# Row pitch and start address of the moved operands in a two-block transformer kernel

## The chip, the cores and the metric

The kernel runs on one core of a Trainium2 chip. The metric is the device time of one execution in microseconds, from the first to the last instruction of the program with what lies around it; the median of several runs is quoted.

## What is computed

Two blocks of transformer layers follow each other on one sequence of 256 tokens and 1024 features, all in float32. The first block has four layers (two pooling mixers, one neighbourhood attention, one convolution) and also carries a context of 256 tokens for a while. The second block has two layers, and each of them is:

```python
x = x + 0.5 * swiglu_ffn(x, ffn1_norm[l], ffn1_w_gate[l], ffn1_w_up[l], ffn1_w_down[l])   # 1024 -> 2816 -> 1024
h = rms_norm(x, mix_norm[l])
aq, ak, av, bq, bk, bv, cq, ck, cv, cg, gates = jnp.split(h @ w_in[l], split_points, axis=-1)
...                                     # three attentions: y_a, y_b, y_c, 512 features each
merged = (g[:, :, 0] * (y_a @ w_branch_a[l]) + g[:, :, 1] * (y_b @ w_branch_b[l])
          + g[:, :, 2] * (y_c @ w_branch_c[l]))
x = x + merged @ w_out[l]
x = x + 0.5 * swiglu_ffn(x, ffn2_norm[l], ffn2_w_gate[l], ffn2_w_up[l], ffn2_w_down[l])
```

## The kernel before

**Three matmuls for one product.** Every large product is made of two parts of each operand. A weight tile (`raw`, 4 rows of 128 by 256 columns, or two such rows) is loaded by a DMA of SP's queue, ScalarE casts it into a high part `whi` (line 162), and VectorE subtracts that from it for a low part `wlo` (line 163). Activations are split in the same way (`split`, lines 341 and 342; `operand`, lines 1157 and 1158). A product of a 128x128 weight square with 256 tokens is then three matmuls of 256 columns that add up in one PSUM half bank: high by high, high by low, low by high (`mm3`; the matmul itself is line 257, called from everywhere). A "triple" below means these three. In the feature-major form (`fm_unit`) the weight square is stationary and the activations are moved: `HH` and `HL`, `UH` and `UL`, `OH` and `OL`. In the token-major form (`tm_unit`, used by `project`) the activations are stationary and the weights `whi`, `wlo` are moved. In the profile's names "mm<-HH,whi" moves HH against stationary whi, and "mm<-whi,HH" moves whi.

**The tiles of activations.** `HH` and `HL` are long-lived tiles of 8 rows (one for each 128 features) of 544 floats, that is 2176 bytes. Columns 0 to 255 of a row hold the normalised input of the layer; columns 288 to 543 are called `YH` and `YL` and hold what the mixers hand to their output product. The first block also uses columns up to 511 (two times 256 tokens) and columns 256 and 257 (a shift). The second block reads 256 columns at a time: all rows of HH in the up products of the feed-forward parts (`ffn`, 22 chunks of 8 rows by 2 squares by 3 matmuls) and in the products of the mixer (`mix`), and four rows of YH for a branch matrix or eight for the output matrix. `UH` and `UL` (22 rows of 256 floats) hold the inner features of a feed-forward part and are moved in its down product; `OH` and `OL` (8 rows of 256 floats) are the same for the last layer of the first block.

**Where they begin.** By the allocator's addresses, modulo 256 bytes: HH and HL begin at 128, so with 2176 bytes a row their rows begin at 128 and 0 in turn, and those of YH at 0 and 128 in turn. UH, UL, OH and OL begin at 0 in every row. The split weights `whi` and `wlo` begin at 192 in every row and square (a tile of 8 floats, `pad_w`, lies ahead of them). Below, "a 0 row" or "a 128 row" is one whose moved operand begins there.

**What sets the order.** The kernel is scheduled by hand. A list `units` holds weight tiles and other work in the order of use. `get` hands out the next tile and lets splits run up to five tiles ahead (`fill`); five raw buffers are loaded ahead of that. Work that hangs on a product (norms, attention steps) is put in by `later` (after so many estimated microseconds of matmuls) and `beside` (steps of a generator at a rate). The second block is `ffn`, `mix`, `ffn` for each of two layers. In a feed-forward part the sums of the norm interrupt the stream of matmuls twice near its start (`norm_a`, `norm_b`); from there to its end it runs through. In the mixer, attention steps stand between chunks of matmuls.

The tiles and the views that are read:

```python
    HH = per.tile([P, KD, 544], F32R, name="HH")
    HL = per.tile([P, KD, 544], F32R, name="HL")
    YH, YL = HH[:, :, 288:544], HL[:, :, 288:544]
    def hx(n):
        return lambda k: HH[:, k, 0:n]
            fp.tile([P, 16], F32, name="pad_u")
            UH = fp.tile([P, KF, 256], F32R, name="UH")
```

Of the kernel before, what the change touches and what calls it, by code (L numbers as in the profile page):

```python
# [114 lines left out]
def kernel(ctx: ExitStack, tc: tile.TileContext, I, csmall, cdec, out):  # L115
# [236 lines left out]
    flip = cst[:, 768:896]  # L352
    ones = per.tile([P, P], F32, name="ones")
    xc = per.tile([P, KD, 512], F32, name="xc")
    HH = per.tile([P, KD, 544], F32R, name="HH")
    HL = per.tile([P, KD, 544], F32R, name="HL")
    par1 = per.tile([P, P], F32, name="par1")
    par2 = per.tile([P, P], F32, name="par2")
    rb = per.tile([P, 512], F32, name="rb")
    rcol = per.tile([P, 4], F32, name="rcol")  # L360
    YH, YL = HH[:, :, 288:544], HL[:, :, 288:544]
    xr = xc[:, :, 0:256]

    PR = {}
# [411 lines left out]
                                       op0=ALU.mult, op1=ALU.add)  # L776

    def hx(n):
        return lambda k: HH[:, k, 0:n]

    def hl(n):
        return lambda k: HL[:, k, 0:n]

    def pool_scale05(pp, j):
        sc05 = pp.tile([P, KD], F32, name="sc05")
# [366 lines left out]

    def operand(j, g):

        for m in range(2):
            ft = 2 * j + m
            A.activation(HH[:, ft, 0:256], xr[:, ft, :], AF.Copy, scale=g[:, ft:ft + 1])
            V.scalar_tensor_tensor(HL[:, ft, 0:256], xr[:, ft, :], g[:, ft:ft + 1], HH[:, ft, 0:256].bitcast(F32),
                                   op0=ALU.mult, op1=ALU.subtract)

    def shift_cols(i):
# [100 lines left out]
    with tc.tile_pool(name="l3", bufs=1) as pp:  # L1262
        sc05 = pool_scale05(pp, 1)
        U = pp.tile([P, KD, 1, 272], F32, name="U")
        SG = pp.tile([P, KD, 256], F32, name="SG")
        pp.tile([P, 24], F32, name="pad_o")
        OH, OL = pp.tile([P, KD, 256], F32R, name="OH"), pp.tile([P, KD, 256], F32R, name="OL")
        pool_edges(U)

        def pool_step(q, outs):  # L1270
            g = 3 - q // 2
            t, col = normed(pp, outs)
            if q % 2 == 0:
                for m in range(2):
                    A.activation(U[:, 2 * g + m, 0, 8:264], t[:, m, :], AF.Identity, bias=col[m])
                pool_means(pp, U, g, 1)

                def rest():
                    if rests.pop(g, None):
                        pool_less(U, g)  # L1280
                        split(YH[:, 2 * g:2 * g + 2, :], YL[:, 2 * g:2 * g + 2, :], U[:, 2 * g:2 * g + 2, 0, 8:264])
                rests[g] = rest
                later(POOL_LATE + POOL_MORE * g, rest)
            else:
                for m in range(2):
                    A.activation(t[:, m, :], t[:, m, :], AF.Identity, bias=col[m])
                sg = SG[:, 2 * g:2 * g + 2, :]
                A.activation(sg, t, AF.Tanh, scale=0.5)
                V.scalar_tensor_tensor(sg, sg, 1.0, t, op0=ALU.add, op1=ALU.mult)

        rests = {}

        def groups(order, bank):
            for g in order:
                rests.get(g, int)()
            pool_groups(pp, 256, lambda ft: (YH[:, ft, :], YL[:, ft, :]), sc05, SG, OH, OL, order, bank)

        def out_half(c, k0):
            fm_unit(outs[c], get(), k0, KD, lambda k: OH[:, k, :], lambda k: OL[:, k, :], 256, None, 4)

        in_chunks(8, pool_step, {4: lambda: groups((3, 2), msb)})
        outs = [two_outs(256) for _ in range(4)]
        out_half(0, 4)
        out_half(1, 4)
        groups((1, 0), msb)
        out_half(2, 4)
        out_half(3, 4)
        for jj in range(4):
            out_half(jj, 0)
            residual(3, jj, outs[jj], 256)  # L1310
            src = xr[:, 2 * jj:2 * jj + 2, :]
            operand(jj, gmul)

            def squares(jj=jj, src=src):
                acc_sq(nrm, ("acc", "sq"), jj, src, 256)
                acc_sq(fnp, ("acc2", "sq"), jj, src, 256, scale=fg[:, 2 * jj:2 * jj + 2])
            later(ACC_LATE, squares)
# [27 lines left out]

    rbb = rb[:, 0:256].unsqueeze(1).to_broadcast([P, 2, 256])

    def residual2(j, gnext, pool):

        if gnext is None:  # L1350
            later(OUT_LATE, lambda: out_tile(j, pool))
        else:
            operand(j, gnext)
            acc_sq(nrm, ("acc", "sq"), j, xr[:, 2 * j:2 * j + 2, :], 256)

    def ffn(na_, nb_, gnext, beside_=None):
        with tc.tile_pool(name="ffn", bufs=1) as fp:
            fp.tile([P, 16], F32, name="pad_u")
            UH = fp.tile([P, KF, 256], F32R, name="UH")
            UL = fp.tile([P, KF, 256], F32R, name="UL")  # L1360
            def up(j, gb, ub):
                t1 = fp.tile([P, 2, 256], F32, tag="t1", bufs=2, name="t1")
                V.tensor_tensor(t1, gb, rbb, op=ALU.mult)
                th = fp.tile([P, 2, 256], F32, tag="th", bufs=2, name="th")
                A.activation(th, t1, AF.Tanh, scale=0.5)
                V.scalar_tensor_tensor(t1, th, 1.0, t1, op0=ALU.add, op1=ALU.mult)
                V.tensor_tensor(t1, ub, t1, op=ALU.mult)  # L1367
                split(UH[:, 2 * j:2 * j + 2, :], UL[:, 2 * j:2 * j + 2, :], t1)

            first = []  # L1370
            later(FF_LATE, na_)
            for j in range(KF // 2):
                gb = fm_bank(KD, hx(256), hl(256))
                if j == 4 and beside_ is not None:
                    beside_()
                if j == 1:
                    flush()
                    nb_()
                    up(*first)
                ub = fm_bank(KD, hx(256), hl(256))  # L1380
                if j:
                    up(j, gb, ub)
                else:
                    first = (j, gb, ub)
            for j in range(4):
                b = fm_bank(KF, lambda k: UH[:, k, :], lambda k: UL[:, k, :])
                y = fp.tile([P, 2, 256], F32, tag="t1", bufs=2, name="t1")
                V.scalar_tensor_tensor(y, b, 0.25, rbb, op0=ALU.mult, op1=ALU.mult)
                xj = xr[:, 2 * j:2 * j + 2, :]
                V.tensor_tensor(xj, xj, y, op=ALU.add)  # L1390
                residual2(j, gnext, fp)
            flush()
# [34 lines left out]
    def mix(l, tabs, nlam, gcol, gnext):  # L1427
        with tc.tile_pool(name="mix", bufs=1) as xp:
# [18 lines left out]


            def project():
                banks = tm_chunk(lambda k, tt: HH[:, k, tt * P:(tt + 1) * P],  # L1450
                                 lambda k, tt: HL[:, k, tt * P:(tt + 1) * P], 2)
                return banks[0].rearrange("p (t f) -> p t f", t=2)

            def scaled(dst, ps, col):
# [99 lines left out]
            def a_gen(qT, kT, v):  # L1554
# [69 lines left out]
                    yield  # L1624
                for hp in range(2):
                    bv = out_features(oA, hp)
                    yh, yl = YH[:, 2 * hp:2 * hp + 2, :], YL[:, 2 * hp:2 * hp + 2, :]
                    A.activation(yh, bv, AF.Copy, scale=gcol[:, 0:1])
                    V.scalar_tensor_tensor(yl, bv, gcol[:, 0:1], yh.bitcast(F32), op0=ALU.mult, op1=ALU.subtract)
                    yield  # L1630

            def b_gen(qT, kT, v):
# [47 lines left out]
                def s3(p):  # L1680

                    b = msb()
                    for q in range(2):
                        for e in range(2):
                            r = slice(64 * e, 64 * e + 64)
                            d = slice(128 * p + 64 * e, 128 * p + 64 * e + 64)
                            mm(b[r, 128 * q:256], v[:, q, d], w_[e][:, 256 * q:256 + 128 * q], q == 0, q == 1)
                    split(YH[:, 4 + p, :], YL[:, 4 + p, :], b[:, 0:256])

                for n in range(6):  # L1690
                    while turned[0] < (6 if n < 2 else 8):
# [15 lines left out]
            def c_gen(qk, v, scg):  # L1707
# [40 lines left out]
                for hp in range(2):  # L1748
                    bv = out_features(oC, hp)
                    y = scratch("ra", [P, 2, 256], 2)  # L1750
                    for q in range(2):
                        h = 2 * hp + q
                        V.scalar_tensor_tensor(y[:, q, :], bv[:, q, :], gcol[:, 4 + h:5 + h], scg[:, h, :],
                                               op0=ALU.mult, op1=ALU.mult)
                    split(YH[:, 2 * hp:2 * hp + 2, :], YL[:, 2 * hp:2 * hp + 2, :], y)
                    yield


# [44 lines left out]
            for i in range(3):  # L1803
# [6 lines left out]
                for j in range(4):  # L1810
# [1 line left out]
                    tg = scratch("z", [P, 2, 256], 4)  # L1812
                    V.tensor_tensor(tg, b, rbb, op=ALU.mult)
                    A.activation(tg, tg, AF.Tanh, scale=0.5)
                    b = fm_bank(4, lambda k: YH[:, y0 + k, :], lambda k: YL[:, y0 + k, :])
                    mj = mg[:, 2 * j:2 * j + 2, :]
                    if i == 0:
                        V.scalar_tensor_tensor(mj, tg, 1.0, b, op0=ALU.add, op1=ALU.mult)
# [3 lines left out]
                    if i == 2:  # L1822
                        for q in ((0,), (1,), (), (2, 3))[j]:
                            o = (2 * q + 4) % 8
                            split(YH[:, o:o + 2, :], YL[:, o:o + 2, :], mg[:, 2 * q:2 * q + 2, :])
            for j in range(4):
                if j % 2 == 0:
                    pair = fm_pair(lambda k: YH[:, (k + 4) % 8, :], lambda k: YL[:, (k + 4) % 8, :])
                for m in range(2):
                    xj = xr[:, 2 * j + m, :]  # L1830
                    V.scalar_tensor_tensor(xj, pair[j % 2][m], 0.5, xj, op0=ALU.mult, op1=ALU.add)
# [39 lines left out]
```

## Time and profile before

| | us |
|---|---|
| median of 3 runs | 1946.94 (1945.92 to 1949.56) |
| the profiled execution | 1944.92 |
| its span, first to last instruction | 1943.1 |
| TensorE busy with matmuls in it | 1880.3 (97%), 14939 matmuls |
| VectorE busy | 1333.2 (69%) |
| ScalarE busy | 923.3 (48%) |
| DMA, mean over the span | 182 GB/s |

A matmul is shown with a modelled end, some 280 ns after its start, although the next one starts earlier; matmuls are pipelined. So neither the busy share nor the mean duration tells how fast they follow each other. That is read from start times (the timeline), or from a piece of the chain of waits that holds nothing but matmuls: its length divided by its count. The mean granted clock of the run is 0.99, and 1.00 from 635 us on.

### The profile page before, as it was taken

The page shows a single profiled execution, that of the slowest core. Times are in us where ns is not written, and L with a number is a line of the kernel's source. Part 1 is how long each engine was busy: PE and PEld are TensorE (multiplying, and loading weights), DVE is VectorE, ACT ScalarE, POOL GpSimd, SP SyncE. Part 2 cuts the span into 40 slices and gives each one's busy share as a digit, 9 for nine tenths or more (in the row PEclk, how much of TensorE's full clock was granted, in tenths as well). Part 3 has the DMA queues.
Part 4 walks back from the last instruction along what each step waited for, and adds up shares of the span by engine and source line. Part 5 has one row for each costly group of instructions (what it writes and reads, how often), then busy time and mean ns, then how long its engine had stood idle before and what let it go on. Part 6 is the DMA issues. An engine that isn't in the chain of part 4 may idle for free.

```text
span 1943.1 us, 36616 instructions
## 1 busy us (share of the span) xinstructions
PE 1880.3 (97%) x14939; PEld 1767.5 (91%) x14939; DVE 1333.2 (69%) x2152; ACT 923.3 (48%) x1509; POOL 123.5 (6%) x194
## 2 busy tenths in 40 slices
PE   7999988889999999999999999999999999999998
PEld 4667876679999999999899999999999989999998
DVE  4655766577787887568867776667656886777654
ACT  3333434445555645446754544444444675454442
POOL 3000421100003100010100000000001000000000
PEclk9999989999999999999999999999999999999999
DMA  8684498865564756565545656565556544555553
GB/s 283 226 273 152 97 218 210 197 191 171 174 194 157 187 174 195 189 200 162 136 151 184 195 174 193 173 196 190 183 190 200 162 138 145 190 191 184 179 190 98
DMA packets 319448, 354.38 MB, mean 182 GB/s; under 512 B 12282, under 2 KB 306416, under 8 KB 319280
## 3 DMA queue, kind: packets, MB, share of 16 engines
q1 hardware_dynamic: 315440, 345.48, 55.5%
q0 software_dynamic: 3648, 6.49, 3.9%
q8 instruction: 117, 1.92, 0.4%
q14 instruction: 51, 0.42, 0.1%
q10 hardware_dynamic: 192, 0.07, 0.0%
HBM read 350.95 MB, written 1.05 MB: 181 GB/s over the span
## 4 chain that ended last, share of the span: by engine, by line
PE 78%; DVE 9%; ACT 6%; DMA 4%; issue 2%; POOL 0%; SPq 0%; DVEq 0%; ACTq 0%; POOLq 0%
PE mm L257 71%; DVE wlo L163 3%; PE sc L257 3%; DMA raw<-in_na_w_in_dram 3%; PE ms L257 2%; ACT whi L162 2%; DMA raw<-in_ada_w_dram 1%; PE mm L1045 1%; ACT pw L1577 1%; DVE ada_acc L554 1%; DVE nt L1202 0%; DVE h_ss L1465 0%; DMA xt<-in_ctx_dram 0%; ACT pw L1658 0%; POOL y L765 0%
## 5 line engine op out<-in xcount | busy, mean ns | idle before, releaser
L257 PE MATMUL mm<-HH,whi 128*128 128x256 f32 (+2 forms) x3000 | 876.8, 292 | 2.2 <-ACT U L875 1.6
L257 PE MATMUL mm<-HL,whi 128*128 128x256 f32 (+2 forms) x3000 | 867.5, 289 | 8.2 <-DVE HL L752 4.1
L257 PE MATMUL mm<-HH,wlo 128*128 128x256 f32 (+2 forms) x3000 | 867.0, 289 | 0.0
L163 DVE TENSOR_TENSOR wlo<-raw,whi 128x1024 fp32r<-128x1024 f32 x564 | 666.4, 1215 | 230.9 <-ACT whi L162 230.4
L162 ACT CAST whi<-raw 128x1024 fp32r<-128x1024 f32 x564 | 561.4, 1032 | 214.0 <-PE mm L257 95.5
L257 PEld LDWEIGHTS mm<-HH,whi 128*128 128x128 f32 x3000 | 566.1, 189 | 29.9 <-issue 15.6
L257 PEld LDWEIGHTS mm<-HL,whi 128*128 128x128 f32 x3000 | 566.0, 189 | 19.7 <-DVE HL L767 5.4
L257 PEld LDWEIGHTS mm<-HH,wlo 128*128 128x128 f32 x3000 | 566.2, 189 | 9.0
L257 PE MATMUL mm<-UL,whi 128*128 128x256 f32 x704 | 196.9, 280 | 0.0
L257 PE MATMUL mm<-UH,whi 128*128 128x256 f32 x704 | 196.9, 280 | 0.0
L257 PE MATMUL mm<-UH,wlo 128*128 128x256 f32 x704 | 196.4, 279 | 0.0
L257 PE MATMUL mm<-whi,HH 128*128 128x256 f32 x640 | 184.0, 287 | 0.0
L257 PE MATMUL mm<-wlo,HH 128*128 128x256 f32 x640 | 178.3, 279 | 2.3 <-DVE wlo L163 2.0
L257 PE MATMUL mm<-whi,HL 128*128 128x256 f32 x640 | 178.0, 278 | 0.0
L257 PEld LDWEIGHTS mm<-UH,whi 128*128 128x128 f32 x704 | 132.3, 188 | 0.0
L257 PEld LDWEIGHTS mm<-UL,whi 128*128 128x128 f32 x704 | 132.0, 188 | 0.0
L257 PEld LDWEIGHTS mm<-UH,wlo 128*128 128x128 f32 x704 | 131.8, 187 | 0.0
L257 PEld LDWEIGHTS mm<-whi,HH 128*128 128x128 f32 x640 | 121.1, 189 | 5.4 <-issue 5.2
L257 PEld LDWEIGHTS mm<-wlo,HH 128*128 128x128 f32 x640 | 121.2, 189 | 3.2 <-DVE wlo L163 3.1
L257 PEld LDWEIGHTS mm<-whi,HL 128*128 128x128 f32 x640 | 120.9, 189 | 0.0
L341 ACT CAST UH<-t 128x512 fp32r<-128x512 f32 x44 | 27.3, 621 | 101.9 <-DVE t L1367 101.9
L554 DVE SCALAR_TENSOR_TENSOR ada_acc<-raw,csil,ada_acc 128x1024 f32<-128x1024 f32 x49 | 64.7, 1320 | 15.8 <-DMA raw<-in_ada_w_dram 15.0
(324 smaller groups left out, 1794.2 us busy)
## 6 DMA issues: line engine op xcount, KB each, us to landing
raw<-in_w_in_dram SPq DMA_DIRECT2D x120, 512.0 KB, 4.4
raw<-in_ada_w_dram SPq DMA_DIRECT2D x96, 512.0 KB, 5.4
raw<-in_ffn_w_gate_dram SPq DMA_DIRECT2D x88, 512.0 KB, 4.8
raw<-in_ffn_w_up_dram SPq DMA_DIRECT2D x88, 512.0 KB, 4.9
raw<-in_ffn_w_down_dram SPq DMA_DIRECT2D x80, 512.0 KB, 4.6
raw<-in_pool_w_in_dram SPq DMA_DIRECT2D x32, 512.0 KB, 5.2
raw<-in_na_w_in_dram SPq DMA_DIRECT2D x32, 512.0 KB, 4.8
raw<-in_conv_w_in_dram SPq DMA_DIRECT2D x32, 512.0 KB, 4.6
```

Source lines behind the costliest of these rows:

```text
L162: A.copy(u.hi, u.raw)
L163: V.tensor_tensor(u.lo, u.raw, u.hi.bitcast(F32), op=ALU.subtract)
L257: T.matmul(o, lhsT=lhsT, rhs=rhs, start=start, stop=stop, skip_group_check=True)
L341: A.copy(hi, src)
L554: V.scalar_tensor_tensor(hold["a"], raw[:, 0, :], cc, hold["a"], op0=ALU.mult, op1=ALU.add)
L1045: T.transpose(b[:, k * P:(k + 1) * P], L[:, k * P:(k + 1) * P], flip)
L1577: A.activation(Lp, Lp, AF.Exp, scale=-1.0, bias=mx[:, q:q + 1], accum_out=sx[:, q:q + 1])
```

## The change

The two activation tiles become plain runs of 8 x 544 floats with two views on the same memory. The first block keeps the view with 544 floats a row. From the end of its last layer on, a second view `HH2`, `HL2` is used: 8 rows of 512 floats, 2048 bytes, in which columns 0 to 255 are the layer's input and columns 256 to 511 are the mixers' output. Which view `operand` writes and `hx`, `hl` read is kept in a small table, switched at the last layer's output and at the start of the second block. The padding tiles ahead of OH and of UH grow by 128 bytes. After it, HH2, HL2, YH2, YL2, UH, UL, OH and OL begin at 128 modulo 256 in every row; the split weights stay at 192. The order of the instructions on every engine and the waits of each are the same before and after.

```diff
-    HH = per.tile([P, KD, 544], F32R, name="HH")
-    HL = per.tile([P, KD, 544], F32R, name="HL")
+    HF = [per.tile([P, KD * 544], F32R, name=nm) for nm in ("HH", "HL")]
...
+    HH, HL = [t.rearrange("p (k c) -> p k c", k=KD) for t in HF]
     YH, YL = HH[:, :, 288:544], HL[:, :, 288:544]
+    HH2, HL2 = [t[:, 0:KD * 512].rearrange("p (k c) -> p k c", k=KD) for t in HF]
+    YH2, YL2 = HH2[:, :, 256:512], HL2[:, :, 256:512]
+    lay = {"read": (HH, HL), "write": (HH, HL)}
...
     def hx(n):
-        return lambda k: HH[:, k, 0:n]
+        return lambda k: lay["read"][0][:, k, 0:n]
...
     def operand(j, g):
+        oh, ol = lay["write"]
         for m in range(2):
             ft = 2 * j + m
-            A.activation(HH[:, ft, 0:256], xr[:, ft, :], AF.Copy, scale=g[:, ft:ft + 1])
-            V.scalar_tensor_tensor(HL[:, ft, 0:256], xr[:, ft, :], g[:, ft:ft + 1], HH[:, ft, 0:256].bitcast(F32),
+            A.activation(oh[:, ft, 0:256], xr[:, ft, :], AF.Copy, scale=g[:, ft:ft + 1])
+            V.scalar_tensor_tensor(ol[:, ft, 0:256], xr[:, ft, :], g[:, ft:ft + 1], oh[:, ft, 0:256].bitcast(F32),
                                    op0=ALU.mult, op1=ALU.subtract)
...
-        pp.tile([P, 24], F32, name="pad_o")
+        pp.tile([P, 56], F32, name="pad_o")
...
             src = xr[:, 2 * jj:2 * jj + 2, :]
+            lay["write"] = HH2, HL2
             operand(jj, gmul)
...
+    lay["read"] = HH2, HL2
...
-            fp.tile([P, 16], F32, name="pad_u")
+            fp.tile([P, 48], F32, name="pad_u")
...
-                banks = tm_chunk(lambda k, tt: HH[:, k, tt * P:(tt + 1) * P],
-                                 lambda k, tt: HL[:, k, tt * P:(tt + 1) * P], 2)
+                banks = tm_chunk(lambda k, tt: HH2[:, k, tt * P:(tt + 1) * P],
+                                 lambda k, tt: HL2[:, k, tt * P:(tt + 1) * P], 2)
...
-                    b = fm_bank(4, lambda k: YH[:, y0 + k, :], lambda k: YL[:, y0 + k, :])
+                    b = fm_bank(4, lambda k: YH2[:, y0 + k, :], lambda k: YL2[:, y0 + k, :])
```

The other hunks replace YH, YL by YH2, YL2 wherever the second block's mixer writes or reads them.

## Rows read from the trace of the kernel before

**Rows 1.** The head of the page.
```profile
span 1943.1 us, 36616 instructions
```

**Rows 2.** Chain of waits, 669 to 1943 us; pieces: start us, us, what.
```profile
by line: PE mm L257 85.7%; DVE wlo L163 1.9%; PE ms L257 1.5%; issue 1.1%; ACT whi L162 1.1%; ACT pw L1577 0.8%; DVE h_ss L1465 0.7%; PE sc L257 0.7%; ACT pw L1658 0.6%; DVE z L1473 0.5%; PE ms L1676 0.5%; ACT z L1456 0.4%; PE sc L1496 0.4%
...
686.38 178.14 PE mm L257 x1524
...
1035.24 91.87 PE mm L257 x780
...
1133.59 179.79 PE mm L257 x1536
...
1319.92 179.17 PE mm L257 x1524
...
1767.17 127.61 PE mm L257 x1092
1895.22 15.55 PE mm L257 x132
```

**Rows 3.** Waits of TensorE, 669 to 1943 us: total us, times, longest.
```profile
PE sc L257 <- ACT qk L1499: 3.1, 2, 1.6
```

**Rows 4.** Busy time of each engine, 1120 to 1305 us.
```profile
1120.00:1305.00 185.00, 185.00 (x1581) 184.95 (x1580) 118.86 (x141) 82.54 (x101) 0.00 (x0) 1.00 0.59 188
```

**Rows 5.** Timeline of TensorE, first feed-forward part: start us, us, what.
```profile
719.83 0.28 PE L257 MATMUL mm<-HH,whi 128*128 128x256 f32 x1
...
740.83 0.28 PE L257 MATMUL mm<-HH,whi 128*128 128x256 f32 x1
```

**Rows 6.** The same, token-major projections of the first mixer.
```profile
869.69 0.28 PE L257 MATMUL mm<-whi,HL 128*128 128x256 f32 x1
...
883.97 0.28 PE L257 MATMUL mm<-whi,HL 128*128 128x256 f32 x1
```

**Rows 7.** Groups by line and shape, VectorE: xcount | busy us, mean ns.
```profile
L1363 DVE TENSOR_TENSOR t<-mm,rb 128x512 f32<-128x512 f32 x44 | 30.1, 685 | 6.1 <-ACT rb L440 6.1
L1813 DVE TENSOR_TENSOR z<-mm,rb 128x512 f32<-128x512 f32 x24 | 16.5, 686 | 5.9 <-PE mm L257 5.9
```

**Rows 8.** By tile: xcount, duration ns min/median/max (HH from 669 us).
```profile
L257 PE MATMUL mm<-HH,wlo x2167: 276/279/286, 668.8 to 1873.3; 128*128 128x256 f32 x197
...
L257 PE MATMUL mm<-UH,whi x704: 279/279/367, 792.6 to 1936.6; 128*128 128x256 f32 x176
...
L257 PE MATMUL mm<-OH,wlo x64: 279/279/282, 640.1 to 665.2; 128*128 128x256 f32 x64
```

**Rows 9.** Timeline of TensorE, seam of a branch product and the next chunk.
```profile
991.85 0.28 PE L257 MATMUL mm<-HH,whi 128*128 128x256 f32 x1
...
992.20 0.28 PE L257 MATMUL mm<-HH,whi 128*128 128x256 f32 x1
...
992.54 0.28 PE L257 MATMUL mm<-HH,whi 128*128 128x256 f32 x1
...
992.88 0.28 PE L257 MATMUL mm<-HH,whi 128*128 128x256 f32 x1
...
993.24 0.28 PE L257 MATMUL mm<-HH,whi 128*128 128x256 f32 x1
```

**Rows 10.** Timeline of TensorE, another such seam.
```profile
1015.87 0.28 PE L257 MATMUL mm<-HH,whi 128*128 128x256 f32 x1
...
1016.23 0.28 PE L257 MATMUL mm<-HH,whi 128*128 128x256 f32 x1
```

**Rows 11.** Timeline of TensorE, first block, 512 columns: ZH at 128, HH at 0.
```profile
145.40 0.39 PE L257 MATMUL mm<-ZL,whi 128*128 128x512 f32 x1
...
150.53 0.39 PE L257 MATMUL mm<-ZH,wlo 128*128 128x512 f32 x1
...
31.15 0.39 PE L257 MATMUL mm<-HL,whi 128*128 128x512 f32 x1
...
32.75 0.40 PE L257 MATMUL mm<-HH,wlo 128*128 128x512 f32 x1
```

More of the change, by code (lines that the diff above doesn't have):

```diff
@@ L778, in hx @@
     def hx(n):
-        return lambda k: HH[:, k, 0:n]
+        return lambda k: lay["read"][0][:, k, 0:n]
     def hl(n):
-        return lambda k: HL[:, k, 0:n]
+        return lambda k: lay["read"][1][:, k, 0:n]
     def pool_scale05(pp, j):
@@ L1626, in a_gen @@
                     bv = out_features(oA, hp)
-                    yh, yl = YH[:, 2 * hp:2 * hp + 2, :], YL[:, 2 * hp:2 * hp + 2, :]
+                    yh, yl = YH2[:, 2 * hp:2 * hp + 2, :], YL2[:, 2 * hp:2 * hp + 2, :]
                     A.activation(yh, bv, AF.Copy, scale=gcol[:, 0:1])
@@ L1687, in s3 @@
                             mm(b[r, 128 * q:256], v[:, q, d], w_[e][:, 256 * q:256 + 128 * q], q == 0, q == 1)
-                    split(YH[:, 4 + p, :], YL[:, 4 + p, :], b[:, 0:256])
+                    split(YH2[:, 4 + p, :], YL2[:, 4 + p, :], b[:, 0:256])
                 for n in range(6):
@@ L1754, in c_gen @@
                                                op0=ALU.mult, op1=ALU.mult)
-                    split(YH[:, 2 * hp:2 * hp + 2, :], YL[:, 2 * hp:2 * hp + 2, :], y)
+                    split(YH2[:, 2 * hp:2 * hp + 2, :], YL2[:, 2 * hp:2 * hp + 2, :], y)
                     yield
@@ L1824, in mix @@
                             o = (2 * q + 4) % 8
-                            split(YH[:, o:o + 2, :], YL[:, o:o + 2, :], mg[:, 2 * q:2 * q + 2, :])
+                            split(YH2[:, o:o + 2, :], YL2[:, o:o + 2, :], mg[:, 2 * q:2 * q + 2, :])
             for j in range(4):
                 if j % 2 == 0:
-                    pair = fm_pair(lambda k: YH[:, (k + 4) % 8, :], lambda k: YL[:, (k + 4) % 8, :])
+                    pair = fm_pair(lambda k: YH2[:, (k + 4) % 8, :], lambda k: YL2[:, (k + 4) % 8, :])
                 for m in range(2):
```

## The prediction

> **What bounds the kernel now.** I read the page first, then the chain of waits, then the waits of TensorE, then start times of single matmuls. The page gives a span of 1943.1 us [rows 1]. The change touches the second block, which begins near 669 us, and one stage just ahead of it; so the chain is read from there on [rows 2]. Of it 85.7% is the line that issues matmuls into the "mm" banks. Only 1.9% is VectorE's weight split, 1.1% ScalarE's. The pieces of the chain say more: single unbroken runs of 780, 1524 and 1536 matmuls, in which nothing but the matmul before released the next. The waits of TensorE in the same stretch are small, the largest sum being 3.1 us [rows 3]. [...] So the second block takes what its matmuls take, one start after another, and the question is what one start to the next costs.
>
> That pace is not one number, although all these matmuls have 256 columns and 128x128 weights. Dividing pieces by their counts: 91.87 / 780 = 117.8 ns, 179.79 / 1536 = 117.05, 15.55 / 132 = 117.8 [rows 2]. By start times: in the up projections of the first feed-forward part, 21.00 us for 180 = 116.67 ns [rows 5]. In the token-major projections of the mixer, 14.28 us for 126 = 113.33 ns [rows 6]. These stages differ in where the moved operand begins, modulo 256 bytes. UH, UL (the 15.55 us piece): always 0. HH, HL as moved operand: 128 and 0 in turn, row by row, because a row is 2176 bytes. The token-major projections move the split weights: always 192. Their stationary side takes turns between 128 and 0 and yet the pace does not change. So address classes go with pace in this trace: 0 at 117.8, 192 at 113.33, and if a 0 row in turn costs what it costs alone, a 128 row in the stretch of rows 5 costs 2 x 116.67 - 117.8 = 115.5. The longer mixer piece (780 at 117.8) has the same rows in the same turns as rows 5 and is slower: the alternation has two steady paces, 116.67 and 117.8, and which one a run falls into was decided at its start.
>
> **The change part by part.**
>
> *Order, waits, amounts of work.* Every engine's instructions stand in the same order with the same waits; only addresses and steps move. Instructions added: none. VectorE and ScalarE write the same shapes; their tiles move by 128 bytes. The nearest rows say that this costs nothing: the same multiply of a PSUM bank by rb takes 685 ns into t1 (which begins at 0) and 686 ns into z (which begins at 224) [rows 7]. I take 0 for them, between -1 and +1 ns on some hundred instructions off the chain, below 0.1 us in sum.
>
> *HH and HL as moved operand, second block.* 2167 triples (hi x hi, hi x lo, lo x hi: the rows of the lo weights count them), 6501 matmuls [rows 8], half of them now at 0. All go to 128. *UH, UL:* 704 triples, 2112 matmuls, from 0 to 128. *OH, OL:* 64 triples, 192 matmuls, from 0 to 128 [rows 8]. The token-major projections keep 192 for what they move: 0.
>
> *The price of a run that is all 128* is not in the trace as a long 256-column run. It is bounded by the few places where two 128 rows follow each other, at the seam of a branch matrix (YH, last row of four) and the next chunk's HH row 0. At 992 us, amid a run at the faster pace, four triples start at 991.85 (0), 992.20 (128), 992.54 (128), 992.88 (0) and end at 993.24 [rows 9]: together 1.39 us. Taking a pair at that pace (0.70) and another 0 triple (0.35) off leaves 0.34 for the second 128 triple, which is also what its first start and the next triple's (992.54, 992.88) give: 0.113 a matmul, the pace of the 192 runs. So one end is 113.33 ns. At 1015 us, amid a run at the slower pace, the second 128 triple starts at 1015.87 and ends at 1016.23 [rows 10]: 0.36 and, with rounding, no less than 0.35, i.e. 117.8 or a little above. That is the other near end. The far end is a wider matmul: with 512 columns, the only long run all at 128 (ZH, ZL in the first layer) takes 5.13 us for 22 = 233.2 ns, while a run all at 0 takes 1.60 us for 7 = 228.6 [rows 11]; there 128 is 2% dearer than 0.
>
> I take 113.33 for the long runs. The reason: in the fast seam the second triple already has the pace of the 192 runs, so a further 128 row meets what the last one met and should stay there; nothing at 0 follows to push it out. At the 113.33 pace:
> - Feed-forward pieces: 178.14 + 179.79 + 179.17 + 127.61 + 2 x 15.55 (a second piece like the one shown follows it) = 695.81 us for 1524 + 1536 + 1524 + 1092 + 264 = 5940 matmuls [rows 2]; 5940 x 0.11333 = 673.2. Gain 22.6 us.
> - Long mixer pieces: 2 x 91.87 (one in each layer) = 183.74 us for 1560 [rows 2]; at the new pace 176.8. Gain 6.9 us.
> - The rest, 6501 + 2112 + 192 - 7500 = 1305 matmuls, mostly in short runs between the attention's own matmuls and in OH. From 116.67 or 117.8 they could gain 3.3 or 4.4 ns each, some 5.2 us; a short run has little time to settle, so I take two thirds, 3.5 us.
>
> Sum: 33.0 us off TensorE's time. All of it is on the chain. What could be late next: the splits and the loads must keep up with a unit of 24 matmuls in 2.72 instead of 2.8 us, 4% more load on engines that are at 64% and 45% there [rows 4]; the token-major stage already runs units at 113.33 in long runs [rows 6], so I take no new wait. Against the profiled run's own time, 1944.92 us with a span of 1943.1, that gives 1911.9; on the median of the three runs, 1946.94, it gives **1914**.
>
> [...] Measured here: the pace depends on the class of the start address, 113.33 against 117.8 at equal columns [rows 2, 6]. [...]
>
> **The rivals.**
> *Half of the runs settle.* The state at a run's start decides, as it does for the alternation now: three of the four feed-forward runs average 116.9 to 117.05 and one 117.57 [rows 2]. If runs with about half of the matmuls stay near 117.8, the gain is about 16 us: **1931**. For: the two seams behave differently [rows 9, 10].
> *All 128 holds the slower pace.* If rows 10 is what an all-128 run does, every matmul takes 117.8. Nothing is gained on UH, OH and the mixer. The feed-forward up projections now at 116.67 lose 1.1 ns: about 1056 matmuls in each of three, 3 x 1.2 = 3.5 us. **1946.9 to 1950.4**.
> *The change makes it slower (all 128 as in the wide matmul).* If 256 columns do at 128 what 512 do, 2% above the pace of 0, a matmul takes about 120 ns [rows 11]. Place: every run of the second block. Price: 3 x 1056 x 3.3 ns = 10.6 us on the fast up projections and 2.2 ns on the remaining 5600, 12.4 us: 23 us, **1970**. It decides from the point where the all-128 pace is above the present mean of the pieces, (695.81 + 183.74) / 7500 = 117.3 ns. Against: the seams show 113.33 and 117.8, neither 120.
> *The change doesn't do what it says.* The address class only goes along with something else (which operand is moved, layer by layer): no change, **1947**. Against: within one stretch, rows of the same tile take different times by their turn [rows 9]. [...]
>
> **How the numbers follow.** Forecast (113.33 in the long runs) 0.42; half settle 0.23; slower pace holds 0.20; as in the wide matmul 0.07; address not the cause 0.08. A measurement of this kernel tells 0.2%, 3.9 us, from no change. Faster: 0.42 + 0.23 = 0.65. Slower: 0.07, and 0.05 of the third case for its upper end: 0.12. Same: 0.23. The range runs from the forecast with all of the short runs and a little more (1946.94 - 36.8 = 1910) to the upper end of the third case (1951); only the wide-matmul case, under 0.1, and the tails are outside. The forecast's own range is 1910 to 1923: up to a quarter of the gain lost to runs that settle late.
>
> **What would show it.** Right: the start-to-start time in the feed-forward runs of HH and UH, 180 matmuls in 20.4 us instead of 21.0 to 21.2; the 780 piece near 88.4 us instead of 91.87; durations of these matmuls at the 276 ns of the token-major rows; first-block stages and token-major paces as before. Half: some pieces at 113.3 and others at 117.8 or in between. Wrong: all pieces at 117.8, or at 120; or the pieces shorter and the waits of TensorE on the weight splits grown by as much, which would mean that the cover on VectorE was not there.

## The result, and the profile after

| | before | after |
|---|---|---|
| median (four runs each) | 1947.65 us | 1921.33 us |
| lowest to highest | 1945.92 to 1949.56 | 1916.45 to 1921.98 |
| the profiled execution | 1944.92 | 1920.95 |
| its span | 1943.1 | 1919.2 |

The ratio of the times is 0.9859, with a 95% interval from 0.984 to 0.9878: 26 us less, where 33 were forecast.

The first line of the page, and of the chain of waits from 660 to 1925 us the shares by line and the long unbroken pieces (start us, us, what), as in [rows 1, 2]:

```profile
span 1919.2 us, 36616 instructions
...
by line: PE mm L257 88.2%; DVE wlo L163 1.5%; PE ms L257 1.5%; ACT whi L162 0.9%; PE sc L257 0.8%; issue 0.8%; ACT pw L1585 0.6%; ACT pw L1666 0.6%; PE ms L1684 0.5%; PE sc L1504 0.5%; DVE h_ss L1473 0.4%; PE mm L1559 0.3%; ACT z L1464 0.2%
...
684.87 179.49 PE mm L257 x1524
867.75 16.96 PE mm L257 x144
...
1035.68 88.42 PE mm L257 x780
...
1130.64 174.09 PE mm L257 x1536
...
1311.27 172.74 PE mm L257 x1524
...
1748.46 123.78 PE mm L257 x1092
1872.68 14.98 PE mm L257 x132
```

Divide each by its count. Three of the four feed-forward runs go at 113.3 ns a matmul (174.09 / 1536, 172.74 / 1524, 123.78 / 1092), and so does the mixer's long piece (88.42 / 780). The first feed-forward run does not: 179.49 / 1524 = 117.8, slower than the 116.9 it had in [rows 2]. The piece of 144 at 867.75 is the token-major projections of the first mixer, at 117.8 where [rows 6] had 113.33. So two things came out otherwise than forecast, and nothing else of size: TensorE's waits did not grow, and VectorE and ScalarE kept up. The largest wait of TensorE (669 to 1925 us; total, times, longest), the busy times in the stretch of [rows 4] (TensorE, weight load, VectorE, ScalarE, GpSimd, granted clock, DMA share, GB/s), and VectorE's multiply into z:

```profile
PE sc L257 <- ACT qk L1507: 2.5, 2, 1.3
...
1120.00:1305.00 185.00, 185.00 (x1632) 184.95 (x1630) 122.10 (x145) 86.24 (x105) 0.00 (x0) 1.00 0.61 195
...
L1821 DVE TENSOR_TENSOR z<-mm,rb 128x512 f32<-128x512 f32 x24 | 16.5, 686 | 1.9 <-PE mm L257 1.7
```

In the same 185 us TensorE now starts 1632 matmuls instead of 1581, 3.2% more, with VectorE at 66% and ScalarE at 47%; the wait is 2.5 us where [rows 3] had 3.1, the multiply takes 686 ns as in [rows 7].

To see every term at once, the times from each matmul's start to the next start were added up, for the 10,392 matmuls of the large products from the first OH matmul on, by what they move (worked out from the start times in the trace):

| moved | matmuls | before, us | after, us | difference |
|---|---|---|---|---|
| HH, HL, YH, YL | 6552 | 775.8 | 757.6 | -18.2 |
| UH, UL | 2112 | 250.8 | 243.8 | -7.0 |
| OH, OL | 192 | 22.6 | 22.6 | 0.0 |
| whi, wlo (token-major) | 1536 | 186.3 | 189.4 | +3.1 |
| sum | | | | -22.1 |

From that first OH matmul to the last matmul the time went from 1299.2 to 1276.9 us, 22.3 less, so these four rows account for it. The part ahead (639.9 against 638.1 us) differs by less than it does among the other profiled executions of this study (638.4 to 642.9).

### The profile page after: what moved, and what is told of

It reads as the page before. It is cut to its first block, busy times and chain, and to the rows that moved or that the text cites. A ratio compares the mean times of both kernels' runs of the same rounds, so it can differ in the third digit from the quotient of the medians.

```text
span 1919.2 us, 36616 instructions
## 1 busy us (share of the span) xinstructions
PE 1858.4 (97%) x14939; PEld 1745.9 (91%) x14939; DVE 1332.1 (69%) x2152; ACT 923.9 (48%) x1509; POOL 124.8 (7%) x194
## 4 chain that ended last, share of the span: by engine, by line
PE 80%; DVE 8%; ACT 6%; DMA 4%; issue 2%; POOL 0%; SPq 0%; DVEq 0%; ACTq 0%; POOLq 0%
PE mm L257 72%; DVE wlo L163 3%; PE sc L257 3%; DMA raw<-in_na_w_in_dram 3%; PE ms L257 2%; ACT whi L162 2%; DMA raw<-in_ada_w_dram 1%; PE mm L1049 1%; DVE ada_acc L558 1%; DVE nt L1207 0%; DMA xt<-in_ctx_dram 0%; ACT pw L1585 0%; ACT pw L1666 0%; POOL y L769 0%; ACT w L1031 0%
```

## The experiments

### One half of the change at a time

The theory after the result: there are two steady paces, 113.3 and 117.8 ns; a run whose moved rows and weight squares are each of one class keeps the pace that it fell into, and the token-major projections are at 113.3 only while their stationary HH squares take turns between 0 and 128. The rival is the prediction's premise, that the class of the moved operand alone sets the pace. Two kernels part the change. In **rows_only** the view with rows of 2048 bytes is kept, and UH, UL, OH, OL stay at 0:

```diff
-        pp.tile([P, 56], F32, name="pad_o")
+        pp.tile([P, 24], F32, name="pad_o")
...
-            fp.tile([P, 48], F32, name="pad_u")
+            fp.tile([P, 16], F32, name="pad_u")
```

**pads_only** is the kernel before with these two pads at 56 and 48: rows of 2176 bytes, but UH, UL, OH, OL at 128.

> The second view with 2048-byte rows, but the padding ahead of UH and OH as before, so that UH, UL, OH, OL begin at 0 as before. Theory (two steady paces, 113.33 and 117.8 ns a matmul; a run whose moved rows and weight squares are all of one class keeps the one it fell into; a run whose weight squares take turns between 0 and 128 while it moves 192 comes to 113.33): HH runs at 113.33 or 117.8 as in the changed kernel, UH at 117.8 whatever came before, token-major runs mostly at 117.8 instead of 113.33 as in the changed kernel. Against the changed kernel (1921.3) UH loses 3 to 4 runs of 528 matmuls x 4.44 ns = 7 to 9 us: 1928 to 1931. Rival (the class of the moved operand alone sets the pace): token-major runs, which move 192 as ever, would not change at all by themselves; HH at one single pace everywhere.

Measured: 1930.4 us (1928.84 to 1930.67), ratio to before 0.9912 (0.9897 to 0.9926), within the 1928 to 1931 expected.

> The padding of the changed kernel, but rows of 2176 bytes as before: UH, UL, OH, OL begin at 128, HH rows at 128 and 0 in turn. Theory: UH runs follow HH runs without a break and take over their state: 113.33 after a 116.67 run, 117.8 after a 117.8 run, so about three of four feed-forward parts gain 528 x 4.44 ns = 2.3 us each, and the three breaks in the last one are new draws: 1938 to 1943. Token-major runs stay at 113.33, because the stationary rows of HH take turns again. Rival (class of the moved operand alone): all UH at one pace; token-major as in the changed kernel (117.8).

Measured: 1942.93 us (1938.56 to 1947.61, ten runs), ratio 0.9975 (0.9965 to 0.9985), within the 1938 to 1943 expected. The gains are 16.8 and 4.2 us against the 1947.17 us that the kernel before took in this comparison; the changed kernel's gain is 26.3. By the sums of start times UH and UL take 250.8 us in rows_only, as before, and 243.8 in pads_only, as in the changed kernel; HH, HL, YH and YL take 759.7 and 776.0. So each half does its own part. In the traces the two nearly add up: from the first OH matmul on, rows_only saves 13.9 us and pads_only 6.7, together 20.6, where three traces of the changed kernel save 22.3 to 23.8. In the medians 16.8 and 4.2 make 21.0 of 26.3; the other 5.3 us have no measured cause.

Pieces of the chain (start us, us, what), then the token-major matmuls by tile (duration ns min/median/max), of rows_only:

```profile
688.04 179.49 PE mm L257 x1524
...
1037.83 88.42 PE mm L257 x780
...
1880.68 15.55 PE mm L257 x132
...
L257 PE MATMUL mm<-whi,HH x512: 276/280/467, 857.5 to 1607.5; 128*128 128x256 f32 x171
```

And of pads_only:

```profile
689.60 175.78 PE mm L257 x1524
...
1036.22 91.87 PE mm L257 x780
...
1318.55 179.16 PE mm L257 x1524
...
1892.99 14.98 PE mm L257 x132
...
L257 PE MATMUL mm<-whi,HH x512: 276/276/469, 855.7 to 1613.2; 128*128 128x256 f32 x171
```

The piece of 132 is UH: 15.55 at 0, 14.98 at 128. The piece of 780 is HH: 91.87 in turns, 88.42 at 128 throughout. The last line of each fence decides between the theory and the rival. The token-major projections move whi and wlo, which begin at 192 in both kernels, yet their median duration is 280 ns in the one and 276 in the other (in streams, below, xda at 113.3 ns shows medians of 276, uad at 117.8 ns 279 and 280), and their sum of start times 189.2 against 186.4 us. What differs is their stationary side: HH's rows all at 128 in rows_only, at 128 and 0 in turn in pads_only. The class of the moved row alone can't be the rule.

The two pieces of 1524 of pads_only show what an entry does. UH follows the HH part of its run without a break. In the first run, 178.14 us before [rows 2], UH gained 2.36 us; in the third, 179.17 before, it gained nothing. By the start times the HH parts of the four runs go at 116.67, 116.67, 117.78 and 116.67 ns, and the UH parts behind them at 113.36, 113.35, 117.77 and 113.38. So UH at 128 takes over the state, faster or slower, in which HH leaves it, as was expected.

### The changed kernel once more

> The changed kernel once more, for a second trace of it. Theory: the same two paces, 340.0 and 353.3 ns a triple, but runs may have drawn differently; if the first feed-forward run (1524 matmuls) falls to 113.33 this time, the time is 6 to 7 us shorter (near 1915), if not, near 1921. Rival (address alone): the same pace in the same places each time, 1921.

Measured: 1923.03 us, and again this piece of the chain:

```profile
688.28 179.50 PE mm L257 x1524
```

The first feed-forward run was slow again, as in rows_only. For the long runs the rival's reading holds: in three traces of the changed kernel (the third is that of after_side, below) each has the same pace at the same place. The short run of OH does not: its sum is 22.6 us in the first trace and 21.8 in the other two, so the same kernel entered it at the slow pace once and at the fast one twice.

### A stream of matmuls alone

To get at the rule, **streams** is a kernel with no layers at all, only the three matmuls of a triple, again and again: 28 patterns of addresses, 48 matmuls each with 256 columns and 128x128 weights, each pattern begun from four different entries (back-to-back transposes; matmuls of one column; a small matmul behind a VectorE copy; a small transpose behind a copy). It computes nothing of the two blocks. The three matmuls move the high rows against the high weights, the low rows against the high weights, and the high rows against the low weights:

```python
    mm(o, lh, rh, kk + k == 0 and m == 0, False)
    mm(o, lh, rl, False, False)
    mm(o, ll, rh, False, kk + k == 7)
```

> The model is left out altogether: the kernel only copies its input and a bank to the output. It runs 28 patterns of operand addresses, each four times in 48 matmuls of 256 columns (triples: high x high, low x high, high x low, 8 rows by 2 squares), every one after a break of its own kind (three transposes; four one-column matmuls; a wait for VectorE; a wait and a transpose). A pattern's PSUM bank has a name: u, then the class of the moved rows and that of the weight squares (a 0, b 64, c 128, d 192); x patterns have moved rows or squares in turn with 128 more; y and z patterns have other classes for the low parts. Theory: every uniform pattern shows the two paces 113.33 and 117.8 by the way it was entered, except where 0 is moved against 192 (uad: 117.8 always, as UH before); xda (moves 192, squares 0 and 128 in turn) comes to 113.33 from every entry; xad shows 116.67 or 117.8. Rival (class of the moved operand alone): all four entries of a pattern alike, and all patterns that move the same class alike.

Measured, ns from start to start at the end of a stream. In the names of the tiles the second letter is the class of the moved rows, the third that of the weights: a, b, c, d for 0, 64, 128, 192. First letter u: both sides uniform; x: one side in turns, row by row or square by square, between its class and 128 further; y: high and low parts of one side 128 apart. Two starts with 24 matmuls between them, for nine streams:

```profile
26.62 0.28 PE L70 MATMUL uaa<-hi,wh 128*128 128x256 f32 x1
29.50 0.28 PE L70 MATMUL uaa<-hi,wh 128*128 128x256 f32 x1
...
95.63 0.28 PE L70 MATMUL uad<-hi,wh 128*128 128x256 f32 x1
98.45 0.28 PE L70 MATMUL uad<-hi,wh 128*128 128x256 f32 x1
...
297.14 0.28 PE L70 MATMUL ucd<-hi,wh 128*128 128x256 f32 x1
299.86 0.28 PE L70 MATMUL ucd<-hi,wh 128*128 128x256 f32 x1
...
303.56 0.28 PE L70 MATMUL ucd<-hi,wh 128*128 128x256 f32 x1
306.39 0.28 PE L70 MATMUL ucd<-hi,wh 128*128 128x256 f32 x1
...
371.74 0.28 PE L70 MATMUL udc<-hi,wh 128*128 128x256 f32 x1
374.56 0.28 PE L70 MATMUL udc<-hi,wh 128*128 128x256 f32 x1
...
422.15 0.28 PE L70 MATMUL xad<-hi,wh 128*128 128x256 f32 x1
424.98 0.28 PE L70 MATMUL xad<-hi,wh 128*128 128x256 f32 x1
...
435.08 0.28 PE L70 MATMUL xad<-hi,wh 128*128 128x256 f32 x1
437.88 0.28 PE L70 MATMUL xad<-hi,wh 128*128 128x256 f32 x1
...
453.49 0.28 PE L70 MATMUL xda<-hi,wh 128*128 128x256 f32 x1
456.21 0.28 PE L70 MATMUL xda<-hi,wh 128*128 128x256 f32 x1
...
646.30 0.28 PE L70 MATMUL ycd<-hi,wh 128*128 128x256 f32 x1
649.02 0.28 PE L70 MATMUL ycd<-hi,wh 128*128 128x256 f32 x1
```

2.88 / 24 = 120.0 ns for uaa, 2.82 to 2.83 / 24 = 117.5 to 117.9 (117.8 over longer stretches) for uad, the second ucd, udc and the first xad, 2.80 / 24 = 116.7 for the other xad, and 2.72 / 24 = 113.3 for the first ucd, xda and ycd. Over all entries of the streams with both sides uniform, by the class of the weights less that of the moved rows:

| weights less moved, modulo 256 bytes | pace, ns | streams |
|---|---|---|
| 0 | 120.0 | 16 of 16 |
| 64 | 113.3 or 117.8, by entry | 9 and 7 |
| 128 | 118.5 to 118.8, two of them 120.0 | 16 |
| 192 | 117.8, one of them 113.3 | 15 and 1 |

The same moved class (128: second letter c) gives 120.0, 117.8, 113.3 or 117.8, and 118.6 or 120.0 with the four classes of weights. So the premise of the prediction, the moved class alone, falls here too. Of the theory, what was said of uad, xda and xad came true; that every other uniform pattern would show the two paces fell: those at distance 64 did, and one entry of udc. (The distance, here and below, is the weights' class less that of the moved rows, modulo 256 bytes.) Beyond the uniform streams: moved rows of one class against weights that take turns between 64 and 192 beyond it (xda, xcd, yda, ycd) went at 113.3 from every entry, 16 of 16. With the distances 64 and 192 made the other way, by moved rows that take turns against weights of one class (xad, xbc, yad, ydc), it was 116.7 to 117.8. Turns between the distances 0 and 128 (xaa, xbd, xca) went at 117.8 to 118.9.

Now the kernels can be read off the streams. Before: HH in turns against 192 is xad, with its two paces 117.8 and 116.7; UH is uad, 117.8; token-major, weights at 192 moved over HH squares in turns, is xda, 113.3. Changed: HH and UH at 128 against 192 are ucd, two paces by entry; token-major is udc, 117.8 from three of four entries. All of these agree with [rows 2, 5, 6] and with the pieces above.

### More patterns

**streams2** is the same kernel with 27 other patterns.

> A stream of matmuls alone, with none of the layers' computation: 27 further patterns of 48 matmuls each, each begun from four entries. Theory (class of the weights less class of the moved rows, modulo 256 bytes): moved rows of one class with weights that take turns between 64 and 192 beyond it, in whichever order, end at 113.3 ns from every entry (moved 128 with high 64 and low 192; moved 64 with squares at 0 and 128 in turn); moved operands that take turns against weights of one class stay at 116.7 to 117.8 as in the first set, also where high and low rows differ; a single odd square or row in four is enough to pull a run to the fast pace, or else the turns must be regular; weights at other distances than multiples of 64 bytes go by the nearest multiple. Rival (only the moved class or only the weights' class counts): the patterns with one moved class all alike, whatever the weights.

What held: squares at 0 and 128 in turn under moved rows at 64 gave 113.3 from all four entries ("wbc"), and fewer odd squares are enough. In "kb" the moved rows are at 128 and the weights at 192, except that the second of the two squares is 128 further. Two of its four entries, 24 matmuls between the two starts of each:

```profile
344.76 0.28 PE L74 MATMUL kb<-hi,wh 128*128 128x256 f32 x1
347.48 0.28 PE L74 MATMUL kb<-hi,wh 128*128 128x256 f32 x1
...
357.48 0.28 PE L74 MATMUL kb<-hi,wh 128*128 128x256 f32 x1
360.22 0.28 PE L74 MATMUL kb<-hi,wh 128*128 128x256 f32 x1
```

2.72 / 24 = 113.3 and 2.74 / 24 = 114.2, the latter with its last triples at 113.3; an odd square in only one row of four ("ka") ends at 113.3 from all entries too. Moved operands whose high and low parts differ, against weights that do not take turns by square, stayed at 117.8 or went to between 120.4 and 121.6, as expected or worse; moved rows in turns against weights at 192 and 64 ("wad") gave 115.5 or 117.8, an odd moved row in four 115.0 or 117.8, and moved parts at 192 and 64 over squares in turns ("wda") 116.7. So none of these serves for the token-major projections together with the other form.

What fell: "in whichever order". With moved rows at 128, high weights at 64 and low at 192 ("yce"), two entries gave 113.3 and two 118.9; with high at 192 and low at 64 (ycd) all four gave 113.3. And "by the nearest multiple of 64" fell: of eleven distances that are no multiple of 64, none gave 113.3 from any entry; 208 and 224 bytes gave 116.7, 112 and 160 bytes 120.0. The two uniform patterns at distance 64 (one of them run twice) again gave both paces, two entries of four each. The kind of entry does not settle which: the third entry of ubc gave 113.3 in streams and 117.8 both times here. A rule for every pattern was not found, only the table for multiples of 64 and the turns.

### A version that should not depend on the entry

The streams say how to take the entry out: high weights at 192, low at 64, moved rows at 128. **lo_far** is the changed kernel with the ring of wlo 128 bytes further, through two pads of 32 floats; two narrow statistics tiles give the room back, so that everything else begins where it did modulo 256 bytes:

```diff
+                wpad.append(wp.tile([P, 32], F32, tag="pad_l", name="pad_l"))
...
+                wpad.append(wp.tile([P, 32], F32, tag="pad_e", name="pad_e"))
...
-        a = sm.tile([P, 32], F32, tag="rs_a", name="rs_a")[:, 0:n]
-        t = sm.tile([P, 32], F32, tag="rs_t", name="rs_t")[:, 0:n]
+        a = sm.tile([P, 16], F32, tag="rs_a", name="rs_a")[:, 0:n]
+        t = sm.tile([P, 16], F32, tag="rs_t", name="rs_t")[:, 0:n]
```

> The changed kernel with the low weights (wlo) 128 bytes further, at 64 modulo 256 bytes, the high ones still at 192, from the first layer to the last; two narrow statistics tiles give the room back, nothing else moves. Moved rows of the second block stay at 128. Theory (what counts is the class of the weights against that of the moved rows; weights that take turns between 64 and 192 beyond the moved class end at 113.3 ns from every entry, as the pattern 'moved 128, high 192, low 64' did): every feed-forward run at 113.3 to 113.4, the first one (1524 matmuls, 179.5 us in the changed kernel) 172.7; the OH stage and the short runs of the mixer at 113.3 too; token-major projections (moved 192 and 64, stationary 128) stay at 117.8. Together 7 to 10 us below the changed kernel, 1911 to 1914 us, if the first block (rows at 0 and 128 in turn) is as before, which no pattern has shown. Rival 1 (the class of the moved rows alone): no fm run changes, 1921 (token-major then moves by half at 64). Rival 2 (a run's pace is drawn anew by chance in each execution): the first run is slow in some executions and fast in others, as before.

Measured: 1917.09 us (1914.91 to 1919.37), ratio to before 0.9852 (0.9836 to 0.9869). Its pieces, and its token-major matmuls by tile:

```profile
685.79 173.10 PE mm L261 x1524
...
1124.64 174.10 PE mm L261 x1536
...
1305.08 173.11 PE mm L261 x1524
...
1742.36 123.78 PE mm L261 x1092
1866.58 15.00 PE mm L261 x132
...
L261 PE MATMUL mm<-whi,HH x512: 276/281/467, 848.8 to 1594.6; 128*128 128x256 f32 x171
```

The mechanism came out as said: the first run takes 173.10 instead of 179.49 us, every feed-forward run is at 113.3 to 113.6, and token-major stays slow (189.9 us). OH's sum is 21.8 us, but the changed kernel reached that too in two of three traces. The first rival, the moved class alone, falls. The second, a pace drawn anew each time, was not seen in the two traces of this kernel. The whole, though, gained less than the 7 to 10 us expected. So it was put beside the changed kernel on one chip:

> The changed kernel again, timed on the same chip and against the same runs of the kernel before as the version with the low weights at 64. Theory (stationary class against moved class; the first feed-forward run has two paces, chosen by how it is entered): about 1921 us, with 4 to 7 us between executions where the first run falls in the slow and in the fast pace; in its profiled execution that run of 1524 matmuls takes 179.5 us (or 172.7 if it was entered at the fast pace), token-major projections at 117.8. Rival (the difference to the version with the low weights at 64 is only that of two chips): the two kernels give the same time here.

> The version with the low weights at 64 again, beside the changed kernel. Theory: 4 to 7 us below the changed kernel of this call, all three long feed-forward runs at 113.3 to 113.6 ns (173 us for 1524), the fourth (1092) at 123.8. Rival: the same time as the changed kernel, or a first run of 179 us.

Measured: the changed kernel 1920.75 us (1918.61 to 1924.94), lo_far 1918.77 (1917.48 to 1920.53). That is 2.0 us less where 4 to 7 were expected, with ranges that overlap, and less than this measurement tells from no change. So that lo_far as a whole is faster is not shown. With the eight runs of each from both comparisons, the medians are 1920.9 and 1918.3. The first feed-forward run, of the changed kernel:

```profile
685.43 179.50 PE mm L257 x1524
```

and of lo_far:

```profile
688.17 173.10 PE mm L261 x1524
```

The run itself is 6.4 us shorter, but it begins 2.7 us later. The first OH matmuls start only 0.2 us apart (639.39 and 639.57), so 2.6 us are lost between them and that run, in the head of the feed-forward part. Two things are seen there. TensorE waits longer for HH rows that ScalarE is still writing: where it pauses for them, one matmul starts 1.36 us after the one ahead instead of 0.74 (the wait is 1.1 instead of 0.5 us). The chain of waits runs through VectorE and ScalarE alone there, in the changed kernel from 655.2 to 668.5 us and in lo_far from 655.2 to 669.6, so a faster TensorE gains nothing. And after the pause for the norm's sum, which is 2.0 us long in both, again from start to start, the matmuls of lo_far go at a granted clock of 0.50 for a while (busy times in two stretches of lo_far, then one of the changed kernel; the number behind the five engines is the granted clock):

```profile
680.40:683.60 3.20, 3.20 (x17) 3.20 (x16) 2.58 (x17) 0.00 (x0) 0.00 (x0) 0.50 0.42 146
677.00:686.00 9.00, 7.27 (x49) 7.08 (x49) 7.84 (x31) 2.08 (x3) 0.00 (x0) 0.81 0.40 124
```

```profile
675.00:684.00 9.00, 7.28 (x64) 7.09 (x64) 7.84 (x32) 2.98 (x4) 0.00 (x0) 1.00 0.53 160
```

In the first line the granted clock is 0.50 and a matmul starts every 0.21 us: some 16 matmuls that cost 0.1 us more each, 1.6 us; the 48 matmuls that follow the norm's sum take 7.21 us in lo_far and 5.57 in the changed kernel. Together with the 0.6 us that makes 2.2 of the 2.6. This drop is not tied to lo_far: between 636 and 700 us the mean granted clock is 0.97 in both executions of lo_far, in rows_only and in the second trace of the changed kernel, and 1.00 in the other two executions of the changed kernel, in pads_only and in the kernel before. What decides it was not found.

## Right and wrong, step by step

**The forecast's case came true in all but two terms.** The time fell by 26 us (1947.65 to 1921.33) where 33 were forecast; it lies within the forecast's own range, 1910 to 1923, near its end.

- *The price of an all-128 run, 113.33:* right for three of four feed-forward runs and both long mixer pieces. The seam of [rows 9] was a good witness. The seam of [rows 10] was one too: it showed the second pace, 117.8, that the same classes also hold. Both were bounds of the price, and the run that stayed slow has exactly the second.
- *Long mixer pieces, -6.9:* 2 x (91.87 - 88.42) = 6.9 us. Right.
- *Feed-forward pieces, -22.6:* 179.49 + 174.09 + 172.74 + 123.78 + 2 x 14.98 = 680.06 against 695.81, that is -15.7. This is the mis-sized term. The step that failed is "a further 128 row meets what the last one met and should stay there": that held for the fast pace, but a run that enters at the slow pace stays there as well. The first run did so in all four profiled executions (three of the changed kernel, one of rows_only); it lost 1.4 us instead of gaining 5.4, and that is 6.8 of the 6.9 us missing here. Why this run, alone of the four, is entered at the slow pace stays open. "Half of the runs settle" named this and set it at half of the matmuls; it was one run of four.
- *The rest, -3.5:* HH, HL, UH, UL and OH, OL together gave -25.2; less 15.7 and 6.9 that leaves -2.6 for the rest. OH gained nothing in the first trace (22.6 us) and 0.8 us in the other two (21.8). A little less than the two thirds taken.
- *Token-major, 0:* wrong, +3.1 us. The step that failed is the reading of [rows 6]: "their stationary side takes turns between 128 and 0 and yet the pace does not change". The turns were what made it fast. With HH uniformly at 128 the projections keep 192 as moved class and still go from about 114 to 117.4 ns on average, pauses left out; streams shows the two cases as xda and udc.
- *VectorE, ScalarE, waits, 0:* right [rows 3, 4, 7], by the lines shown above; the rate of matmuls rose by 3.2%, a little less than the 4% more load that the prediction allowed for.

The premise under all of this, "address classes go with pace" by the moved operand, was half of the truth. It gave the right number because the weights' class, 192, was the same everywhere in the trace of before: 192 - 128 = 64 against 192 - 0 = 192. A trace in which only one operand's address varies can't tell "this address" from "this address less that one". That this did no harm is in part luck: by the premise, 192 with its 113.33 was as good a place for the moved rows as 128, and against weights at 192 that is udd, 120.0 ns from all four entries. The seam of [rows 9] pointed to 128. The two misses, the first run and the token-major projections, both went against the gain, so the time did not come near the forecast by errors that cancel. Of the rivals, "slower pace holds" is what the first run alone does; "as in the wide matmul" (120 ns) was in no run of this kernel, though 120.0 ns exists, where weights and moved rows share a class. "Address not the cause" is out: the streams differ in nothing but addresses. 113.3, 116.7, 117.8, 118.6 and 120.0 ns were measured there at one column count, 256, with nothing changed but the two addresses and the entry.

What stays open: which property of an entry chooses between 113.3 and 117.8 at a distance of 64, why the order of 64 and 192 between high and low weights matters (ycd against yce), what chooses the pace of token-major (udc had one entry of four at 113.3), and the paces at distances that are no multiple of 64. Why the difference of the two addresses counts, no run here shows.

## What to carry to other kernels

When long runs of equal matmuls follow each other at different paces, divide unbroken pieces of the chain by their counts and look at both operands' start addresses modulo 256 bytes, the weights' less the moved rows'. Here, with both sides uniform, equal classes were the worst (120.0 ns at 256 columns). Moved rows of one class with weights that take turns between 64 and 192 beyond it were the best, 113.3 from every entry, whether the turns went square by square or the high weights stood at 64 beyond and the low ones at 192; with high and low the other way round (yce) two of four entries stayed at 118.9. A layout that suits one form of a product can spoil the form in which the roles are swapped (here the token-major projections lost 3.1 us), so price every place where a moved tile serves as the stationary side as well. And a pace that is kept once entered has to be counted run by run, not as a mean (1524 matmuls took 179.49 us in the first run, 172.74 in the third).

## What the runs showed of the hardware that was not expected

- The pace depends on the weights' start address relative to the moved rows', by up to 6% in the uniform streams (113.3 to 120.0 ns), with a mean granted clock of 0.999 in that run.
- At a distance of 64 bytes it has two steady values for the same instructions, 113.3 and 117.8; 1524 matmuls in a row do not leave the slow one (179.49 us), a run that follows without a break takes over the one ahead of it (UH behind HH in pads_only), and with one weight square in four at another class ("ka") all four entries ended at 113.3.
- The same wait of TensorE, 1.7 us for the norm's sum at the head of the second block, was followed by a stretch at a lower granted clock in both executions of lo_far (0.81 over 9 us) and not in two of the changed kernel (1.00); in the kernel before the wait was 1.5 us and the granted clock stayed at 1.00.
